# Six half-size weight tiles, one line for loads and crossings in the planner, a third U bank, and half of x over the crossbar

## The chip, the cores and the metric

The kernel runs on one core of a Trainium2 chip. The metric is device time of one execution in microseconds (us). The core has a matrix engine (PE, with its weight loads listed as PEld), a vector engine (DVE), an activation engine (ACT), a small-vector engine (POOL), and a queue engine (SP) that issues most transfers. ACT issues transfers too. A *crossing* below is a transfer that transposes 16-bit data on its way from one on-chip buffer to another.

## The reference

A four-layer decoder trunk over 256 tokens of width 1024, all in float32. Each layer has a token mixer of its own kind, then a gated feed-forward block, then a gated per-layer embedding:

```
for i in range(4):
    h = rmsnorm(x, ln_mix_pre[i])
    y = (rglru_block, dilated_attention, stick_breaking_attention, differential_attention)[i](h)
    x = x + rmsnorm(y, ln_mix_post[i])
    h = rmsnorm(x, ln_ffn_pre[i])
    x = x + rmsnorm((silu(h @ w_in[:, :2816]) * (h @ w_in[:, 2816:])) @ w_out, ln_ffn_post[i])
    gate = sigmoid(x @ w_ple_gate[i] + b_ple_gate[i])
    x = x + rmsnorm(gate * (p[i] @ w_ple_proj[i]), ln_ple[i])
```

The mixers have 16 heads of 64 (the fourth pairs them into 8); all projections are 1024 wide, qkv 3072. About 233 MB of weights are read once.

## The kernel before

**Two halves.** The tokens are split into two halves of 128 rows. Each half is a generator (`half(0)`, `half(1)`) that walks through all four layers and asks for weight slices one after another. Half 1 runs `LAG` = 11 slices behind half 0, so that one half's matmuls can fill the time in which the other normalises, transposes or takes its softmax.

**Weights.** A chunk is 1 MB of weights: four slices of 128 x 512. A raw tile holds one chunk, and there are `RAWRING` = 3 raw tiles. `Weights.load` starts the transfers of chunks ahead: column chunks of one or two pieces, row chunks in one transfer of 1 MB, the last row chunk of a matrix in two. `Weights.ensure` works by units of half a chunk (two slices): ACT copies the unit rounded to the fast matmul format into a `hi` tile, DVE subtracts to get a `lo` tile, and a ring of `RING` = 9 such pairs feeds the matmuls. A product is three matmuls of 512 columns: hi x hi, hi x lo, lo x hi (`mm3`). A raw tile is free for the next chunk when both of its units are split. Two chunks (`NATIVE`) are not split.

**Transposes of x.** `to_hT` needs x with the feature on the partition, as eight blocks of 128 x 128, and is called 22 times: before each of three attentions, four feed-forward blocks and four embeddings, for both halves. Blocks 0 to `XX` - 1 go over PE (`split_T`: matmuls with the identity into a `psT` bank), the others two at a time over the crossbar (`cross_T`: DVE copies the 16-bit halves apart into `planes`, ACT or SP issues the transposing transfer into `turned`, DVE copies back). `parts` then makes hi (ACT) and lo (DVE) of each block. With `XX` = 6, blocks 0 to 3 are one PE group, blocks 4 and 5 a second, and blocks 6 and 7 one crossing. Gated activations (`GBY`) and x (`XBY`) cross from ACT's queue, attention weights (`PBY`) from SP's.

**PSUM.** There are eight banks: four in `psY` (outputs), two in `psU` (products on their way: gated columns, q and k, v, attention outputs, the embedding's projection), two in `psT` (transposes).

**Order.** All instructions are recorded first, with their dependences, and `schedule` then plans an order for every engine by list scheduling over 24 rounds. Its prices are in `price` and `delay`; `Wires.land` says when a transfer lands. Before, a crossing issued by ACT lands 5250 ns after its start and takes no room; one from SP moves the shared line to at least 3750 ns after its start and adds 450; plain loads share that line.

Of the kernel before, what the change touches and what calls it, by code (L numbers as in the profile page):

```python
# [11 lines left out]
F32 = mybir.dt.float32  # L12
# [8 lines left out]
P = 128  # L21
# [11 lines left out]
LAG = 11  # L33
LOOK = 2
RING = 9
RAWRING = 3
PIECES = ((0, 256), (256, 512), (512, 1024))
LAST_PIECES = ((0, 512), (512, 1024))
WARM = 26
XX = 6  # L40
XQK = 0
XP = 4
GBY = 0
# [7 lines left out]
NATIVE = (0, 6)  # L51
# [198 lines left out]

XBAR_ISSUE = 1250
XBAR_LAND = 4000

# [14 lines left out]
class Wires:  # L270
# [3 lines left out]
        self.busy = 0.0  # L274

    def land(self, eng, op, t, size):
        if op == "dma_start_transpose":
            if eng == "ACT":
                return t + XBAR_ISSUE + XBAR_LAND
            self.busy = max(self.busy, t + XBAR_ISSUE + XBAR_LAND - 1500) + 450  # L280
            return self.busy + 1050
        self.busy = max(self.busy, t + DMA_FIRST) + size / DMA_RATE
        return self.busy + DMA_TOLD

# [33 lines left out]
def delay(a, b, op=None):  # L318

    if op == "dma_start_transpose":  # L320
        return XBAR_LAND
    if a == "SP":
# [99 lines left out]
class Weights:  # L422
# [29 lines left out]

        self.add("rows_n", w[k0 * P:(k0 + 2) * P, :].rearrange("(k p) n -> p k n", p=P))

    def load(self, upto):
        while self.nraw <= upto and self.nraw < len(self.chunks):
            if self.nraw in NATIVE:
                self.nraw += 1
                continue
            kind, what = self.chunks[self.nraw]  # L460
            r = self.raw_pool.tile([P, 4, 512], F32, tag="raw", name=f"raw{self.nraw}")
            if kind == "cols":
                for off, n, ap in what:
                    self.nc.sync.dma_start(out=r[:, :, off:off + n], in_=ap)
            elif kind == "rows":
                self.nc.sync.dma_start(out=r.rearrange("p (k c) n -> p k (c n)", k=2), in_=what)
            else:
                for c in range(2):
                    self.nc.sync.dma_start(out=r[:, 2 * c:2 * c + 2, :], in_=what[:, :, c * 512:(c + 1) * 512])
            self.raw[self.nraw] = r  # L470
            self.nraw += 1

    def ensure(self, slot, look=LOOK):
        last = min(slot // 2 + look, 2 * len(self.chunks) - 1)
        while self.nunit <= last:
            u = self.nunit
            self.nunit += 1
            self.units.pop(u - RING, None)
            if u // 2 in NATIVE:

                t = self.split_pool.tile([P, 2, 512], F32, tag="hi")
                for off, n, ap in self.chunks[u // 2][1]:
                    self.nc.sync.dma_start(out=t[:, :, off:off + n], in_=ap[:, 2 * (u % 2):2 * (u % 2) + 2, :])
                self.units[u] = (t, None)
                continue
            self.load(u // 2 + RAWRING - 1)
            r = self.raw[u // 2][:, 2 * (u % 2):2 * (u % 2) + 2, :]
            hi = self.split_pool.tile([P, 2, 512], F32R, tag="hi", name=f"hi{u}")
            lo = self.split_pool.tile([P, 2, 512], F32R, tag="lo", name=f"lo{u}")
            self.nc.scalar.copy(out=hi, in_=r)  # L490
            self.nc.vector.tensor_tensor(out=lo, in0=r, in1=hi, op=ALU.subtract)
            self.units[u] = (hi, lo)
# [6 lines left out]
def trunk(ctx, tc, a, out):  # L499
    nc = Program(tc)  # L500
    sb = ctx.enter_context(tc.tile_pool(name="sb", bufs=1))
    ps = ctx.enter_context(tc.tile_pool(name="ps", bufs=1, space=PSUM))
    pool = lambda name, bufs, real=sb: Ring(nc, name, bufs, real)
    cp = pool("cp", 1)
    raw_pool = pool("rawp", RAWRING)
    split_pool = pool("splitp", RING)
    gp = pool("gp", 3)
    ap = pool("ap", 1)
    tp_ = pool("tp", 2)
    psY = pool("psY", 4, ps)  # L510
    psU = pool("psU", 2, ps)
    psT = pool("psT", 2, ps)
    wp = pool("wp", 1)


# [111 lines left out]
    for i in range(DEPTH):  # L627
        if i == 0:
            add_out(a["a_w_out"][0], KT)
        else:  # L630
            n = "abcd"[i]
# [40 lines left out]
    def split_T(src, hi, lo, nblk, g=None):  # L672

        t = psT.tile([P, 512], F32, tag="t")
        for b in range(nblk):
            TE.transpose(t[:, b * P:(b + 1) * P], src[:, b * P:(b + 1) * P], ident)
        parts(t[:, 0:nblk * P].rearrange("p (b c) -> p b c", c=P), hi, lo, g)
# [19 lines left out]
    def to_hT(h, g=None):  # L697

        hi, lo = alloc_hT(h)
        gk = lambda k: None if g is None else g[:, k]  # L700
        for k0 in range(0, XX, 4):
            k = slice(k0, min(k0 + 4, XX))
            split_T(x[h][:, k.start * P:k.stop * P], hi[:, k, :], lo[:, k, :], k.stop - k0, gk(k))
        for k0 in range(XX, KT, 2):
            k = slice(k0, k0 + 2)
# [619 lines left out]
```

## Time and profile before

| | |
|---|---|
| median of 3 runs | 1306.0 us (1304.79 to 1307.13) |
| profiled execution, its own time | 1309.04 us |
| span of the profile | 1307.2 us |
| mean granted PE clock | 0.998 |
| PE busy | 1285.9 us, 98% |
| DVE busy | 992.4 us, 76% |
| ACT busy | 755.4 us, 58% |
| read from memory | 233.92 MB, 180 GB/s over the span |

The profiled execution ran 1.84 us longer than the span from its first to its last instruction. A busy PE is not PE at its peak: matmuls overlap in the records, and small pauses between them are counted in. What a stage is short of is read from windows of time and from the waits, not from the shares over the whole span.

### The profile page before, as it was taken

The numbers are of one execution on the slowest core, as the hardware profiler recorded it, in microseconds if no ns is written. First come the engines' busy times: TensorE is split into PE (matmuls) and PEld (weight loads), VectorE is DVE, ScalarE is ACT, GpSimd is POOL, SyncE is SP. The second block draws the span as 40 slices with busy tenths as digits, with TensorE's granted clock in tenths as the row PEclk, the third lists the DMA queues.
The fourth block names the chain that finished last, engine by engine and source line by source line (L and its number), as shares of the span: only waits on it lengthen the run. The fifth ranks groups of instructions, "written<-read, shape, count | busy, mean of one in ns | idle before, by whom it ended". The sixth has DMA issues, their size and how long they took to land.

```text
span 1307.2 us, 16953 instructions
## 1 busy us (share of the span) xinstructions
PE 1285.9 (98%) x6062; PEld 1033.0 (79%) x6062; DVE 992.4 (76%) x1760; ACT 755.4 (58%) x1300; POOL 35.6 (3%) x62
## 2 busy tenths in 40 slices
PE   9999999999999999999999999999999999999997
PEld 8977888887777888888777788888877777888886
DVE  7999666689986766668888876666889878666675
ACT  8985444466865644445667564444567766444453
POOL 1000000001000000000000000000000000000000
PEclk9999999999999999999999999999999999999999
DMA  9368677676678866667667777667666558667661
GB/s 346 125 207 219 207 208 203 204 214 201 166 203 184 229 204 198 199 206 232 199 162 173 195 222 209 202 196 203 222 199 189 141 151 230 209 209 205 205 195 36
DMA packets 257332, 258.37 MB, mean 198 GB/s; under 512 B 99296, under 2 KB 216288, under 8 KB 257248
## 3 DMA queue, kind: packets, MB, share of 16 engines
q1 hardware_dynamic: 197408, 242.86, 60.6%
q10 hardware_dynamic: 59840, 14.43, 6.7%
q8 instruction: 47, 0.77, 0.3%
q14 instruction: 37, 0.30, 0.1%
HBM read 233.92 MB, written 1.05 MB: 180 GB/s over the span
## 4 chain that ended last, share of the span: by engine, by line
PE 70%; DVE 13%; DMA 7%; ACT 7%; issue 2%; POOL 0%; SPq 0%; ACTq 0%; POOLq 0%; DVEq 0%
PE psU_u_n L178 43%; PE psY_y_n L178 26%; DVE splitp_lo_n L178 5%; DVE w_n L178 4%; DMA xp_turned_n<-xp_planes_n 4%; ACT w_n L178 2%; ACT splitp_hi_n L178 2%; DMA rawp_raw_n<-in_a_w_in_dram 2%; DVE ap_t_n L178 1%; ACT L178 1%; PE psT_t_n L178 1%; DVE cp_x_n L178 1%; DVE xp_planes_n L178 1%; DVE ap_hTlo_n L178 1%; DMA rawp_raw_n<-in_c_w_qkv_dram 1%
## 5 line engine op out<-in xcount | busy, mean ns | idle before, releaser
L178 DVE TENSOR_TENSOR splitp_lo_n<-rawp_raw_n,splitp_hi_n 128x1024 fp32r<-128x1024 f32 x420 | 511.5, 1221 | 165.7 <-ACT splitp_hi_n L178 162.7
L178 ACT CAST splitp_hi_n<-rawp_raw_n 128x1024 fp32r<-128x1024 f32 x420 | 436.3, 1046 | 213.7 <-PE psU_u_n L178 124.7
L178 PE MATMUL psU_u_n<-splitp_hi_n,ap_hThi_n 128*128 128x512 f32 x992 | 395.1, 399 | 1.5 <-ACT ap_B_n L178 1.1
L178 PE MATMUL psU_u_n<-splitp_lo_n,ap_hThi_n 128*128 128x512 f32 x992 | 393.9, 397 | 0.0
L178 PE MATMUL psU_u_n<-splitp_hi_n,ap_hTlo_n 128*128 128x512 f32 x992 | 392.5, 397 | 0.1
L178 PEld LDWEIGHTS psU_u_n<-splitp_hi_n,ap_hThi_n 128*128 128x128 f32 x992 | 186.9, 188 | 49.2 <-issue 3.5
L178 PEld LDWEIGHTS psU_u_n<-splitp_hi_n,ap_hTlo_n 128*128 128x128 f32 x992 | 186.5, 188 | 45.5 <-DVE ap_hTlo_n L178 1.4
L178 PEld LDWEIGHTS psU_u_n<-splitp_lo_n,ap_hThi_n 128*128 128x128 f32 x992 | 186.9, 188 | 43.6 <-DVE splitp_lo_n L178 0.5
L178 PE MATMUL psY_y_n<-splitp_hi_n,y_n 128*128 128x512 f32 x352 | 137.1, 395 | 0.7 <-ACT y_n L178 0.7
L178 PE MATMUL psY_y_n<-splitp_hi_n,w_n 128*128 128x512 f32 x352 | 133.3, 397 | 0.0
L178 ACT ACTIVATE w_n<-psU_u_n,tp_sm_n 128x256 f32<-128x256 f32 (+1 forms) x96 | 47.2, 491 | 126.4 <-PE psU_u_n L178 81.1
L178 DVE SCALAR_TENSOR_TENSOR w_n<-psU_u_n,tp_sm_n,w_n 128x256 f32<-128x256 f32 x88 | 42.4, 483 | 64.1 <-ACT w_n L178 64.1
L178 PE MATMUL psY_y_n<-splitp_hi_n,ap_hThi_n 128*128 128x512 f32 x208 | 82.7, 401 | 1.2 <-DVE y_n L178 1.1
L178 PE MATMUL psY_y_n<-splitp_lo_n,ap_hThi_n 128*128 128x512 f32 x208 | 82.3, 398 | 0.0
L178 DVE COPY w_n<-xp_turned_n 128x512 uint16<-128x512 uint16 x150 | 68.1, 457 | 18.3 <-DMA xp_turned_n<-xp_planes_n 18.3
L178 PE MATMUL psY_y_n<-splitp_hi_n,ap_hTlo_n 128*128 128x512 f32 x208 | 80.7, 397 | 0.0
L178 PEld LDWEIGHTS psY_y_n<-splitp_hi_n,y_n 128*128 128x128 f32 x352 | 66.0, 188 | 17.1 <-ACT y_n L178 1.1
L178 PEld LDWEIGHTS psY_y_n<-splitp_hi_n,w_n 128*128 128x128 f32 x352 | 65.9, 188 | 15.4 <-DVE w_n L178 0.2
L178 PE MATMUL psY_y_n<-splitp_lo_n,w_n 128*128 128x512 f32 x176 | 70.0, 398 | 0.0
L178 PE MATMUL psY_y_n<-splitp_lo_n,y_n 128*128 128x512 f32 x176 | 69.3, 394 | 0.0
L178 DVE COPY xp_planes_n<-w_n 128x512 uint16<-128x512 uint16 x148 | 61.5, 423 | 4.9 <-DMA xp_turned_n<-xp_planes_n 1.4
L178 POOL TENSOR_TENSOR tp_sm_n<-tp_sm_n,cp_half_neg_n 128x1 f32<-128x1 f32 (+1 forms) x44 | 31.5, 716 | 1130.3 <-DVE tp_sm_n L178 1130.3
(149 smaller groups left out, 1384.5 us busy)
## 6 DMA issues: line engine op xcount, KB each, us to landing
rawp_raw_n<-in_w_ffn_in_dram SPq DMA_DIRECT2D x176, 512.0 KB, 4.9
rawp_raw_n<-in_w_ffn_out_dram SPq DMA_DIRECT2D x40, 1024.0 KB, 4.9
rawp_raw_n<-in_w_ple_gate_dram SPq DMA_DIRECT2D x16, 1024.0 KB, 5.0
rawp_raw_n<-in_b_w_qkv_dram SPq DMA_DIRECT2D x16, 512.0 KB, 4.8
rawp_raw_n<-in_c_w_qkv_dram SPq DMA_DIRECT2D x16, 512.0 KB, 4.9
rawp_raw_n<-in_d_w_qkv_dram SPq DMA_DIRECT2D x16, 512.0 KB, 4.7
rawp_raw_n<-in_a_w_in_dram SPq DMA_DIRECT2D x6, 1024.0 KB, 9.5
rawp_raw_n<-in_w_ffn_out_dram SPq DMA_DIRECT2D x8, 512.0 KB, 4.7
```

Source lines behind the costliest of these rows:

```text
L178: getattr(engine.real, op)(*[self.bind(v) for v in args], **{k: self.bind(v) for k, v in kw.items()})
```

## The change

A raw tile now holds one unit (512 KB) instead of a chunk, and there are six instead of three: the same memory. `load` is replaced by `fetch(u, t)`, which starts the transfers of unit `u`, and is used for the unsplit units too; `ensure` fetches up to five units ahead of the one that it splits. A column chunk's piece of 512 KB becomes two of 256 KB, a row chunk of 1 MB two of 512 KB. `XX` becomes 4: blocks 4 and 5 of x go over the crossbar as blocks 6 and 7 do. `psU` gets three banks and `psT` one. In the planner every crossing, of either queue, starts on the shared line no sooner than 1180 ns after its issue, holds it for 870 ns, and is told 1700 ns later; the backward pass keeps its old prices.

```
-RAWRING = 3
+RAWRING = 6
-XX = 6
+XX = 4
+XBAR_FIRST, XBAR_TAKES = 1180, 870
+XBAR_TOLD = 1700
...
         if op == "dma_start_transpose":
-            if eng == "ACT":
-                return t + XBAR_ISSUE + XBAR_LAND
-            self.busy = max(self.busy, t + XBAR_ISSUE + XBAR_LAND - 1500) + 450
-            return self.busy + 1050
+            self.busy = max(self.busy, t + XBAR_FIRST) + XBAR_TAKES
+            return self.busy + XBAR_TOLD
...
+    def fetch(self, u, t):
+
+        kind, what = self.chunks[u // 2]
+        j = u % 2
+        if kind == "cols":
+            for off, n, ap in what:
+                self.nc.sync.dma_start(out=t[:, :, off:off + n], in_=ap[:, 2 * j:2 * j + 2, :])
+        elif kind == "rows":
+            self.nc.sync.dma_start(out=t.rearrange("p c n -> p (c n)"), in_=what[:, j, :])
+        else:
+            self.nc.sync.dma_start(out=t, in_=what[:, :, j * 512:(j + 1) * 512])
...
-            self.load(u // 2 + RAWRING - 1)
-            r = self.raw[u // 2][:, 2 * (u % 2):2 * (u % 2) + 2, :]
+            while self.nraw < min(u + RAWRING, units):
+                if self.nraw // 2 not in NATIVE:
+                    self.raw[self.nraw] = self.raw_pool.tile([P, 2, 512], F32, tag="raw", name=f"raw{self.nraw}")
+                    self.fetch(self.nraw, self.raw[self.nraw])
+                self.nraw += 1
+            r = self.raw.pop(u)
...
-    psU = pool("psU", 2, ps)
-    psT = pool("psT", 2, ps)
+    psU = pool("psU", 3, ps)
+    psT = pool("psT", 1, ps)
```

## Rows read from the trace of the kernel before

**Rows 1.** The page: span, and busy time of each engine.

```profile
span 1307.2 us, 16953 instructions
PE 1285.9 (98%) x6062; PEld 1033.0 (79%) x6062; DVE 992.4 (76%) x1760; ACT 755.4 (58%) x1300; POOL 35.6 (3%) x62
```

**Rows 2.** Stretches of 20 us; the first row names the columns.

```profile
core 0: us, PE busy (x) PEld busy (x) DVE busy (x) ACT busy (x) POOL busy (x), PEclk, DMA share, GB/s
0.00:20.00 20.00, 17.53 (x128) 17.09 (x129) 13.09 (x37) 14.31 (x26) 3.88 (x12) 1.00 0.90 325
140.00:160.00 20.00, 20.00 (x88) 16.09 (x87) 12.83 (x18) 9.07 (x12) 0.00 (x0) 1.00 0.64 191
300.00:320.00 20.00, 19.23 (x87) 15.30 (x86) 19.52 (x38) 13.47 (x25) 2.26 (x2) 1.00 0.63 201
320.00:340.00 20.00, 19.63 (x105) 15.13 (x104) 19.30 (x61) 17.11 (x49) 0.93 (x1) 1.00 0.58 174
420.00:440.00 20.00, 20.00 (x91) 16.12 (x90) 15.96 (x30) 14.32 (x26) 1.10 (x2) 1.00 0.71 198
640.00:660.00 20.00, 18.08 (x83) 14.46 (x83) 15.09 (x32) 12.73 (x30) 1.25 (x2) 0.91 0.69 196
700.00:720.00 20.00, 18.77 (x115) 14.15 (x115) 19.69 (x37) 14.44 (x24) 0.38 (x2) 1.00 0.67 146
960.00:980.00 20.00, 19.37 (x89) 15.42 (x88) 19.63 (x38) 13.48 (x26) 1.41 (x2) 1.00 0.63 197
1040.00:1060.00 20.00, 18.88 (x94) 14.31 (x93) 19.00 (x54) 14.32 (x43) 1.01 (x1) 1.00 0.89 184
```

**Rows 3.** The chain that ended last, in a feed-forward block: start, us, what.

```profile
114.92 9.78 PE psU_u_n L178 x42
...
131.70 9.80 PE psU_u_n L178 x42
```

**Rows 4.** The same chain: two PE transposes of x between matmuls.

```profile
616.81 0.22 PE psT_t_n L178 x2
```

**Rows 5.** Groups by line and tile: DVE's two copies of a crossing (count, busy us, mean ns).

```profile
L178 DVE COPY xp_planes_n<-cp_x_n 128x512 uint16<-128x512 uint16 x22 | 9.3, 421 | 0.1
L178 DVE COPY w_n<-xp_turned_n 128x512 uint16<-128x512 uint16 x150 | 68.1, 457 | 18.3 <-DMA xp_turned_n<-xp_planes_n 18.3
```

**Rows 6.** Waits of PE's weight loads: us in total, times, longest.

```profile
PEld psU_u_n L178 <- ACT ap_B_n L178: 2.5, 3, 1.3
PEld psU_u_n L178 <- DVE ap_t_n L178: 2.3, 2, 1.2
PEld psU_u_n L178 <- DVE ap_hTlo_n L178: 1.4, 4, 0.5
PEld psU_u_n L178 <- ACT w_n L178: 0.7, 2, 0.4
```

**Rows 7.** The chain that ended last: two loads on it in layer 2.

```profile
635.89 7.50 DMA rawp_raw_n<-in_c_w_qkv_dram
...
711.76 6.33 DMA rawp_raw_n<-in_c_w_out_dram
```

**Rows 8.** The tile `turned`: ACT's issues of crossings (min/median/max ns), and landings of all.

```profile
L178 ACTq DMA_TRANSPOSE xp_turned_n<-xp_planes_n x110: 1205/1207/2197, 89.8 to 1279.9; - x110
...
DMA to landing us min/median/max: 2.3/3.5/8.9
```

**Rows 9.** Transfers by line: count, KB each, median us from issue to landing.

```profile
rawp_raw_n<-in_w_ffn_in_dram SPq DMA_DIRECT2D x176, 512.0 KB, 4.9
rawp_raw_n<-in_w_ffn_out_dram SPq DMA_DIRECT2D x40, 1024.0 KB, 4.9
```

**Rows 10.** The raw tile: SP's issues of one matrix's loads (min/median/max ns).

```profile
L178 SPq DMA_DIRECT2D rawp_raw_n<-in_w_ffn_in_dram x176: 367/499/1536, 74.5 to 1221.9; - x176
```

**Rows 11.** What SP's queue waited for: us in total, times, longest.

```profile
SPq L178 <- DVE splitp_lo_n L178: 524.5, 118, 12.8
```

**Rows 12.** The chain that ended last: a crossing of attention weights in layer 1.

```profile
391.07 8.90 DMA xp_turned_n<-xp_planes_n
```

More of the change, by code (lines that the diff above doesn't have):

```diff
@@ L453, in add_rows_n @@
         self.add("rows_n", w[k0 * P:(k0 + 2) * P, :].rearrange("(k p) n -> p k n", p=P))
[L455 to L471, printed above, removed]
+    def fetch(self, u, t):
[8 more added lines that the diff above has]
+            self.nc.sync.dma_start(out=t, in_=what[:, :, j * 512:(j + 1) * 512])
     def ensure(self, slot, look=LOOK):
-        last = min(slot // 2 + look, 2 * len(self.chunks) - 1)
+        units = 2 * len(self.chunks)
+        last = min(slot // 2 + look, units - 1)
         while self.nunit <= last:
@@ L481, in ensure @@
                 t = self.split_pool.tile([P, 2, 512], F32, tag="hi")
-                for off, n, ap in self.chunks[u // 2][1]:
-                    self.nc.sync.dma_start(out=t[:, :, off:off + n], in_=ap[:, 2 * (u % 2):2 * (u % 2) + 2, :])
+                self.fetch(u, t)
                 self.units[u] = (t, None)
                 continue
-            self.load(u // 2 + RAWRING - 1)
-            r = self.raw[u // 2][:, 2 * (u % 2):2 * (u % 2) + 2, :]
+            while self.nraw < min(u + RAWRING, units):
[4 more added lines that the diff above has]
+            r = self.raw.pop(u)
             hi = self.split_pool.tile([P, 2, 512], F32R, tag="hi", name=f"hi{u}")
```

## The prediction

> **What bounds the kernel now.** Begin with the page. PE is busy 98% of the span, DVE 76% [rows 1]: whatever is gained has to be gained on PE's own time or in the few places where PE stands. Then cut the time into stretches. In the feed-forward blocks PE is busy 20.00 of 20 us while DVE and ACT have 13 and 9 [rows 2]; the chain there is matmuls alone, and repeats every 16.78 us for 48 + 24 = 72 matmuls of 512 columns, 0.233 us each [rows 3]. No edit of buffers or transfers shortens that. The pauses are where a layer begins or its attention runs: PE lacks 0.77 and 0.37 us in the first two stretches of layer 1, 0.63 in layer 3, with DVE at 19.3 to 19.6 of 20; 1.92 and 1.23 us in layer 2; 1.12 us late in layer 3 [rows 2]. So the change can act on three things: work that PE no longer does, waits that end in a load or a crossing, and waits for a free U bank. Against them stands what it adds to DVE, ACT and the transfer engines.
>
> All terms are set against the profiled execution's 1309.04 us (1307.2 of span and 1.84 around it). That run lies 3.0 us above the median of 1306.0, so the sum is carried over to the median as a difference. About 0.2% (2.6 us) is what a measurement of this kernel can tell from no change.
>
> **PE work removed.** 22 calls of `to_hT` each lose two PE transposes. Two take 0.22 us on the chain [rows 4], so 22 x 0.22 = 4.8 us. Where DVE is the short engine, PE time saved buys nothing: I take out the six calls ahead of attention and the two of layer 0, and count 14 x 0.22 = 3.1. Bounds: 0 and 4.8.
>
> **DVE work added.** Each call gains one crossing, so a copy apart of 0.421 and a copy back of 0.457 us [rows 5], 0.88 us; hi and lo of the blocks are made as before. With DVE at 13 to 16 of 20 us this is covered by PE's matmuls. Where DVE is at 19.3 or more (layers 1 and 3, two calls each) the cover is gone: 4 x 0.88 = 3.5; with layer 0's two calls 5.3. PE still has 96 to 98% there [rows 2], so a DVE delay is paid only in part. I take +2.6, half of the upper bound; bounds 0 and 5.3.
>
> **The crossing's latency and its issue.** Blocks 4 and 5 are wanted two slices, 2 x 3 x 0.233 = 1.4 us, before blocks 6 and 7, which already cross today. On ACT's queue the second crossing stands behind the first, whose issue takes 1.21 us [rows 8]; what waits behind both is ACT's `hi` copies, the sum of squares for the norm, and then DVE. So a call's last block may be 1.4 + 1.2 = 2.6 us tighter. The eight feed-forward calls have the least cover, since the other half then has only its lag of 11 slices left: upper bound 8 x 2.6 = 20.8 us. Lower bound nothing: today PE's weight loads for U wait only 1.4 us in all, four times, for the `lo` of x [rows 6], and the stretch in which half 1 of layer 1 enters its block shows PE at 20.00 [rows 2]. I take +2.0, near the rows.
>
> **Raw tiles.** SP's queue sits waiting for DVE's split 524.5 us in 118 waits [rows 11]: a load is issued when a raw tile comes free, not when the line is free. Today the tile comes free after its second unit; half tiles come free after each, and a unit no longer waits for the other unit's bytes. Where this counts is layer 2: a load of 7.50 us stands on the chain, issued late behind DVE, and one of 6.33 us before the output projection [rows 7]. The first costs PE 1.92 us of standing, and behind it the granted clock of that stretch is 0.91 [rows 2]: 0.09 x 20 = 1.8 us more, PE running for 3.6 us at 1.2 instead of 2.4 GHz after it stood. The second is in the stretch that lacks 1.23 us. Together 4.9 us is the upper bound of the gain, 0 the lower (another wait right behind). I take -3.5: the tile is free about one split sooner, and half the bytes land first; what is late next is DVE's own queue. The price is more transfers: the 176 loads of one matrix become 352, at 0.50 us of SP's queue each [rows 10], 88 us more, spread over a queue that waits six times as long. Crossings of attention weights queue on SP too, so a load that waits for its tile holds them up, as it does now.
>
> **The planner's line.** Crossings land after 3.5 us in the median, at worst 8.9 [rows 8]; the old model says 5.25 for ACT's, unloaded or not. The long ones stand on the chain: 8.90 us in layer 1 [rows 12], and the stretch late in layer 3 lacks 1.12 us at a transfer share of 0.89 [rows 2]. A plan that puts loads and crossings in one line places fewer consumers ahead of what they wait for. Upper bound of the gain: 2 x 1.12 = 2.2, the second 1.12 for layer 1's spot. A new order can also be worse by about as much. I take -1.0.
>
> **PSUM.** Three rows of PE's waits for U name the evictions that free a bank: `v` by ACT (2.5), the embedding's product by DVE (2.3), ACT's copies (0.7), 5.5 us in all [rows 6]. A third bank removes the cause; some of the time goes to DVE, which is behind in the same stretches. I take -3.5; bounds 0 and 5.5. The single `psT` bank I cost at nothing: with four PE blocks x fills one bank where six filled two, so a call of `to_hT` leaves no fewer banks than now. If that doesn't hold, x and the other half's q and k queue for the one bank, and each waits for the other's evictions on ACT and DVE.
>
> **Sum.** -3.1 + 2.6 + 2.0 - 3.5 - 1.0 - 3.5 = -6.5 us: 1302.5 for the profiled execution, 1299.5 for the median, 0.5% less.
>
> **The rivals.**
> *Slower: x arrives late.* The eight feed-forward calls show their full latency, because half 1's lag doesn't grow with it. The sign turns where a call costs (6.5 + 2.0) / 8 = 1.06 us instead of the 0.25 that I take. At 1.7 us, two thirds of the 2.6, it is 13.6 - 8.5 = +5.1: 1311. For it: the second issue of 1.21 us and the crossing's worst landing of 8.9 [rows 8]. Against it: 1.4 us of waits in all today [rows 6]. The Trainium skill, in "VectorE: DVE Perf Modes" (Rules for kernel authors), says to transpose 128 x 128 on TensorE where PSUM will do as the destination, and to use the crossbar otherwise; by it this edit goes the wrong way, and no row here shows the two paths side by side for the same block.
>
> *The same: smaller transfers carry less.* In the first 20 us 325 GB/s go at a share of 0.90, 361 at a full share; in the feed-forward block, with pieces of 512 KB in short rows, 191 at 0.64, 298 at a full share [rows 2], 17% less. If halving the pieces cost the same again, the start, where the share is 0.90, would need 20 / 0.83, 4.1 us more; the steady part, at 0.64, would hide it. Then -6.5 + 4.1 = -2.4: 1303.6. Against it: 512 KB and 1024 KB land in the same 4.9 us [rows 9], so size isn't what they wait for. The Trainium skill's "DMA: Bandwidth & Descriptors" (Rules for kernel authors) asks for at least 1 MiB per transfer for the best bandwidth, and the change goes from there to 512 and 256 KB; by the landings in the trace the rule doesn't bite between 512 and 1024 KB, and 256 KB is not shown.
>
> *The same: the next wait takes the place.* Loads and U banks are freed, but DVE, at 19.3 to 19.6 of 20 in those stretches [rows 2], is what ends last anyway: the two terms of -3.5 fall away, and +0.5 remains: 1306.5.
>
> *All of it.* Every term at its better bound: -4.8 - 4.9 - 2.2 - 5.5 = -17.4, nothing paid: 1288.6.
>
> **How the numbers follow.** The forecast gets 0.48, "all of it" 0.14, smaller transfers 0.08, the next wait 0.12, x late 0.18. So faster 0.62, same 0.20, slower 0.18. The forecast's own range is 1295 to 1303; the range given goes from 1290, which leaves out about half of "all of it", to 1310, which leaves out the worse half of the late x.
>
> **What would show it.** Right: in layer 2's first stretch PE near 20 and its clock at 1.00; no 7.50 us load on the chain; waits of U for `v`, the embedding's product and ACT's copies under 2 us together; 44 transposes of x fewer; the matmuls' period unchanged at 16.78 us. Wrong: PE standing at the start of the feed-forward blocks behind a `lo` or `hi` of x; DVE's share at 20 in layers 1 and 3 with PE lower than today; the first weights later than now; PE's transposes waiting for evictions of `psT`.

## The result and the profile after

| | before | after |
|---|---|---|
| median | 1306.4 us (4 runs beside those of after) | 1315.0 us (1313.7 to 1316.8, 4 runs) |
| ratio | | 1.0065, 95% interval 1.0048 to 1.0082 |
| forecast | | 1299.5, range 1290 to 1310 |

The kernel became 8.7 us slower; the prediction has the wrong sign and its range doesn't hold the time. The profiled execution of after took 1316.8 us.

The page of after, its span and busy time [rows 1]:

```profile
span 1315.0 us, 17797 instructions
PE 1285.8 (98%) x6018; PEld 1027.2 (78%) x6018; DVE 1005.9 (76%) x1804; ACT 753.5 (57%) x1298; POOL 36.9 (3%) x62
```

PE issues 44 instructions fewer, and DVE 44 more: these are the transposes that went and the two copies of 22 crossings, as predicted. DVE's busy time grew by 13.5 us. PE's busy time is the same although it has less to do, and the span is 7.8 us longer: what grew is time in which PE stands or runs slowly. The period of a feed-forward block did not move (16.78 us before [rows 3]); the chain that ended last has it at 16.76 us, six rounds in 100.53:

```profile
797.44 9.78 PE psU_u_n L178 x42
...
897.97 9.78 PE psU_u_n L178 x42
```

Stretches of 20 us, where PE lost and where it won (0 to 20, 640 to 660 and 700 to 720 stand in [rows 2] for before):

```profile
core 0: us, PE busy (x) PEld busy (x) DVE busy (x) ACT busy (x) POOL busy (x), PEclk, DMA share, GB/s
0.00:20.00 20.00, 16.75 (x125) 16.26 (x126) 12.66 (x36) 14.50 (x27) 4.08 (x12) 1.00 0.91 326
100.00:120.00 20.00, 17.41 (x75) 13.10 (x73) 16.48 (x38) 10.26 (x20) 0.66 (x1) 1.00 0.79 184
260.00:280.00 20.00, 18.62 (x82) 14.64 (x81) 13.64 (x24) 10.85 (x17) 0.55 (x1) 1.00 0.76 178
...
440.00:460.00 20.00, 18.68 (x81) 14.72 (x79) 14.74 (x25) 11.30 (x19) 0.55 (x1) 1.00 0.90 225
600.00:620.00 20.00, 18.60 (x82) 14.71 (x82) 15.82 (x25) 11.25 (x21) 0.55 (x1) 1.00 0.64 187
...
640.00:660.00 20.00, 19.52 (x92) 14.90 (x90) 17.62 (x32) 13.93 (x27) 1.41 (x2) 1.00 0.77 225
700.00:720.00 20.00, 20.00 (x119) 15.38 (x118) 18.77 (x41) 16.06 (x29) 0.80 (x3) 1.00 0.80 227
```

Before, the four stretches of loss were:

```profile
100.00:120.00 20.00, 19.33 (x87) 15.22 (x86) 18.42 (x52) 12.16 (x21) 0.55 (x1) 1.00 0.83 210
260.00:280.00 20.00, 20.00 (x91) 16.12 (x90) 16.41 (x25) 12.11 (x19) 0.55 (x1) 1.00 0.67 211
440.00:460.00 20.00, 20.00 (x87) 16.00 (x86) 14.15 (x23) 9.74 (x14) 0.00 (x0) 1.00 0.85 236
600.00:620.00 20.00, 20.00 (x94) 16.16 (x93) 18.65 (x31) 12.05 (x21) 1.10 (x2) 1.00 0.84 256
```

Layer 2 is mended as predicted: 640 to 660 went from 18.08 to 19.52 and its clock from 0.91 to 1.00, and 700 to 720 from 18.77 to 20.00. The new losses lie elsewhere, at the seams of the stages: where half 1 enters its block in layer 0 (100 to 120), in layer 1's block (440 to 460), and where a block passes into the embedding (260 to 280, 600 to 620). DVE is far from full there, 13.6 to 16.5 of 20. So no engine became the bound; something stands.

What stands shows in the list of waits (us in total, times, longest), here rows of DVE, ACT and PE's weight loads:

```profile
DVE w_n L178 <- DMA xp_turned_n<-xp_planes_n: 36.7, 39, 3.0
...
PEld psT_t_n L178 <- DVE cp_x_n L178: 7.0, 6, 1.8
...
ACT y_n L178 <- DMA w_n<-in_p_dram: 6.0, 4, 1.6
...
ACT w_n L178 <- DMA w_n<-in_p_dram: 4.2, 3, 2.6
...
PEld psU_u_n L178 <- ACT ap_hThi_n L178: 3.8, 8, 1.8
PEld psU_u_n L178 <- DVE ap_hTlo_n L178: 3.4, 8, 0.9
...
PEld psU_u_n L178 <- ACT ap_B_n L178: 1.6, 5, 0.4
...
PEld psU_u_n L178 <- ACT w_n L178: 0.7, 2, 0.4
```

Two of these waits, before:

```profile
DVE w_n L178 <- DMA xp_turned_n<-xp_planes_n: 18.3, 15, 3.7
...
ACT w_n L178 <- DMA w_n<-in_p_dram: 0.5, 1, 0.5
```

DVE's wait for a crossing to land, ahead of the copy back, doubled: 18.3 us in 15 waits, now 36.7 in 39. The crossings themselves land no later: 2.3/3.6/8.6 us least, median and most, where it was 2.3/3.5/8.9 [rows 8]. DVE arrives at them sooner. One such place is the timeline of DVE from 108 to 115 us; the bracket is idle time and what ended it:

```profile
108.46 0.20 DVE L178 TENSOR_SCALAR w_n<-w_n 128x64 f32<-128x64 f32 x1
110.30 0.45 DVE L178 COPY w_n<-xp_turned_n 128x512 uint16<-128x512 uint16 x1 [1.64 <-DMA xp_turned_n<-xp_planes_n]
110.65 1.21 DVE L178 TENSOR_TENSOR splitp_lo_n<-rawp_raw_n,splitp_hi_n 128x1024 fp32r<-128x1024 f32 x1
111.78 0.42 DVE L178 TENSOR_TENSOR y_n<-w_n,y_n 128x256 fp32r<-128x256 f32 x1
113.83 0.84 DVE L178 COPY w_n<-xp_turned_n 128x512 uint16<-128x512 uint16 x2 [1.63 <-DMA xp_turned_n<-xp_planes_n]
```

DVE works through its list in order. The first stand is for a gated crossing, and behind it waits a weight split that doesn't need it; the second is for x's own two crossings, whose copies go into the `hi` and `lo` that follow. ACT had issued all three in a row from 103.86 us on. PE shows the bill at once: from one matmul's start to the next it takes 1.61 us at 109.63, where it waits for the gated product itself, and 1.71 us at 113.06, where it waits for a `hi` of x, instead of 0.233.

The second wait is ACT's for the plain load of `p`, the embedding's input: 0.5 us before, 10.2 in the two rows now. It stands ahead of the seams into the embedding. In 260 to 280 us ACT, DVE and PE have, in this order:

```profile
273.41 0.41 ACT L178 CAST y_n<-w_n 128x256 fp32r<-128x256 f32 x1 [1.62 <-DMA w_n<-in_p_dram]
...
276.27 1.54 DVE L178 SCALAR_TENSOR_TENSOR cp_x_n<-ap_t_n,tp_sm_n,cp_x_n 128x256 f32<-128x256 f32 x3
...
276.81 0.83 PE L178 MATMUL psT_t_n<-ident,cp_x_n 128*128 128x128 f32 x4 [1.38 <-DVE cp_x_n L178]
```

Behind ACT's copy of `p` stands the sum of squares for the norm that ends the block, behind that DVE's update of x, and PE's transposes wait for x. The same happens in the other three layers (1.40, 0.74 and 1.23 us of PE; 4.75 us in all four). In these four places `p` lands 4.1 to 4.9 us after its issue, where before it took 2.1 to 2.2.

### The profile page after: what moved, and what is told of

It reads as the page before. It is cut to its first block, busy times and chain, and to the rows that moved or that the text cites. A ratio compares the mean times of both kernels' runs of the same rounds, so it can differ in the third digit from the quotient of the medians.

```text
span 1315.0 us, 17797 instructions
## 1 busy us (share of the span) xinstructions
PE 1285.8 (98%) x6018; PEld 1027.2 (78%) x6018; DVE 1005.9 (76%) x1804; ACT 753.5 (57%) x1298; POOL 36.9 (3%) x62
## 4 chain that ended last, share of the span: by engine, by line
PE 41%; DVE 4%; DMA 3%; ACT 2%; issue 1%; POOL 0%; ACTq 0%; POOLq 0%; DVEq 0%; SPq 0%
PE psU_u_n L178 27%; PE psY_y_n L178 13%; DMA xp_turned_n<-xp_planes_n 2%; DVE splitp_lo_n L178 2%; DMA w_n<-in_p_dram 1%; DVE w_n L178 1%; PE psT_t_n L178 1%; ACT splitp_hi_n L178 1%; DVE cp_x_n L178 1%; DVE xp_planes_n L178 0%; ACT w_n L178 0%; POOL tp_sm_n L178 0%; DVE ap_hTlo_n L178 0%; DVE ap_t_n L178 0%; ACT ap_hThi_n L178 0%
## 5 line engine op out<-in xcount | busy, mean ns | idle before, releaser
L178 DVE COPY w_n<-xp_turned_n 128x512 uint16<-128x512 uint16 x172 | 78.6, 459 | 37.2 <-DMA xp_turned_n<-xp_planes_n 36.7
L178 PEld LDWEIGHTS psY_y_n<-splitp_hi_n,y_n 128*128 128x128 f32 x352 | 66.1, 188 | 17.9 <-ACT y_n L178 1.7
```

The costliest lines, as they stand in the source:

```text
L178: getattr(engine.real, op)(*[self.bind(v) for v in args], **{k: self.bind(v) for k, v in kw.items()})
```

## The experiments

The expectations call the theories by short names. PROMISE says that the new line in the planner promises landings sooner than the chip delivers them, so that the order puts waiting copies ahead of work that is ready. BUF says that x's second crossing waits for a landing buffer shared with the gated crossings. The others are named in the texts. All ratios are against the kernel before.

**The four parts, each alone.** `only_tiles` has the changed `Weights` class and six raw tiles. `only_x`, `only_line` and `only_psum`:

```
-XX = 6
+XX = 4
```
```
-            if eng == "ACT":
-                return t + XBAR_ISSUE + XBAR_LAND
-            self.busy = max(self.busy, t + XBAR_ISSUE + XBAR_LAND - 1500) + 450
-            return self.busy + 1050
+            self.busy = max(self.busy, t + XBAR_FIRST) + XBAR_TAKES
+            return self.busy + XBAR_TOLD
```
```
-    psU = pool("psU", 2, ps)
-    psT = pool("psT", 2, ps)
+    psU = pool("psU", 3, ps)
+    psT = pool("psT", 1, ps)
```

> The kernel before with the six half tiles alone. The prediction's term: -3.5 us, 1302 to 1304. Theory SP (the pauses ahead of the embedding come from the p load queued on SP behind a raw load that waits for its tile): slower by 3 to 7 us, with ACT waiting over 1 us for p at each of the four layers. Theories LINE and X: within 2 us of before, p within 0.5 us of ACT's need.

Measured: 1302.3 us, 0.9974 (0.996 to 0.9987).

> The kernel before with half of x over the crossbar alone. The prediction's terms together: -3.1 + 2.6 + 2.0 = +1.5 us. Theory X (the second crossing and its place in ACT's queue are the loss): slower by 5 to 10 us, with PE's waits for the hi and lo of x going from some 3 to over 8 us. Theories SP and LINE: within 3 us of before.

Measured: 1320.2 us, 1.0103 (1.0086 to 1.012).

> The kernel before with the planner's new line alone. The prediction's term: -1.0 us. Theory LINE (crossings of ACT's queue are promised 3.75 us after issue instead of 5.25, and DVE, which works in order, stands more behind those that land late): slower by 3 to 8 us, DVE's waits for crossings going from 18 us to 35 or more. Theories SP and X: within 2 us of before.

Measured: 1306.8 us, 1.0003 (0.9994 to 1.0013).

> The kernel before with three U banks and one T bank alone; x still takes two groups of PE transposes, now through one bank. The prediction's term: -3.5 us, waits of U's weight loads for v, the embedding's product and ACT's copies going from 5.5 to under 2 us. A rival, the single T bank as the loss: slower by 2 us or more, 1.2 us of it ahead of the first product, with PE transposes waiting for evictions of T.

Measured: 1303.6 us, 0.9977 (0.9964 to 0.9989).

Added up, -4.3 + 13.6 + 0.2 - 3.0 = +6.5 (medians against the 1306.6 of before in these runs): x would be the culprit, and the line harmless. Theory LINE fell for the line alone, whose DVE waits are 22.6 us and not 35; so did theory SP (`p` behind raw loads) for the tiles alone: ACT waits 2.6 us for `p`, and the time fell. Rows of PE's weight loads in `only_x` point at x too:

```profile
PEld psU_u_n L178 <- DVE ap_hTlo_n L178: 6.7, 10, 2.2
PEld psU_u_n L178 <- ACT ap_hThi_n L178: 6.1, 5, 2.9
...
PEld psY_y_n L178 <- ACT ap_hThi_n L178: 2.9, 5, 1.3
...
PEld psY_y_n L178 <- DVE ap_hTlo_n L178: 0.4, 2, 0.2
```

They add up to 16.1 us of waits for hi and lo of a transposed input, where before had 1.4 us for `lo` at U [rows 6] and 1.7 us for both at the outputs.

**The whole without x.** The counter-test:

```
-XX = 4
+XX = 6
```

> The changed kernel with x back to six blocks on PE. If the parts add up: 1306.5 - 3.4 (tiles) - 3.0 (PSUM) + 0.2 (line) = 1300. If the parts only look good alone, and what slows the changed kernel is their joint order: 1305 or more.

Measured: 1316.0 us, 1.0076 (1.0058 to 1.0094). With x back on PE the time is as bad as with the whole change. My reading of the four single runs fell: the parts don't add.

**What x costs by itself.** `x_twice` keeps `XX` = 6 and issues a crossing of blocks 4 and 5 besides, whose result isn't used; `x_own` is `only_x` with landing tiles of x's own; `x_early` is `only_x` with the second half of x updated first.

```
+        for k0 in range(4, XX, 2):
+            t = s256("gg").rearrange("p (b t) -> p b t", b=2)
+            cross_T(x[h][:, k0 * P:(k0 + 2) * P], t, by=(A, nc.sync)[XBY])
```
```
-            t = s256("gg").rearrange("p (b t) -> p b t", b=2)
+            t = wp.tile([P, 256], F32, tag="xown", bufs=2).rearrange("p (b t) -> p b t", b=2)
```
```
-PIECES = ((0, 256), (256, 512), (512, 1024))
+PIECES = ((512, 1024), (0, 256), (256, 512))
```

> The kernel before; blocks 4 and 5 of x go over PE as before and are used from there, and go over the crossbar too, into a tile that nobody reads. Theory WORK (DVE's two copies, ACT's issue, the transfer, the buffers they take): slower by 8 to 14 us, as with half of x over the crossbar. Theory LATE (the blocks come too late for the matmuls): within 4 us of before. Theory BUF (the landing tile's ring of two, shared with the gated columns and p): slower by 5 to 14 us, since the tile is taken all the same.

Measured: 1312.0 us, 1.004 (1.0025 to 1.0056).

> Half of x over the crossbar alone, but the crossings of x land in two tiles of their own instead of the ring of two that the gated columns and p use. Theory BUF: most of the 13.6 us come back, 1306 to 1311. Theories LATE and WORK: 1317 to 1322, no change.

Measured: 1318.7 us, 1.0094 (1.0077 to 1.0111).

> Half of x over the crossbar alone, but the update of x writes its second half first, so that the crossings can start some 1.0 us sooner and the PE blocks come last. Theory LATE: 3 to 8 us of the 13.6 come back, 1312 to 1317, and PE's waits for hi and lo of x fall from 16 to under 12 us. Theories WORK and BUF: 1318 to 1322.

Measured: 1322.3 us, 1.0117 (1.0067 to 1.0167).

The crossing as added work costs 5.3 us (1312.0 - 1306.65), between what WORK and LATE expected; buffers of its own give back 1.6 of 13.6, so BUF falls; an earlier second half shows no gain, and its runs spread from 1313.9 to 1328.8. No theory came out whole. What the three kernels with half of x on the crossbar share is that PE waits longer for hi and lo of a transposed input than the 3.1 us of before: 16.1 us, 11.9 with buffers of its own, 17.9 with the earlier half. `x_twice`, where nothing waits for the added crossing's result, has 8.2.

**Which pairs.** Half tiles with the PSUM part; the change without the line:

```
-            self.busy = max(self.busy, t + XBAR_FIRST) + XBAR_TAKES
-            return self.busy + XBAR_TOLD
+            if eng == "ACT":
+                return t + XBAR_ISSUE + XBAR_LAND
+            self.busy = max(self.busy, t + XBAR_ISSUE + XBAR_LAND - 1500) + 450
+            return self.busy + 1050
```

> Half tiles and PSUM's banks, without the planner's line and without more of x on the crossbar. Theory PROMISE (with small loads on the line the planner promises ACT's crossings after 3.8 us instead of 5.25, the chip delivers as before, and what waits in order behind them stands): the two gains of 3.4 and 3.0 add up, 1299 to 1302. Rival DRAW (every edit only draws another order, good or bad by up to 8 us): anything from 1298 to 1314, most likely 1304 to 1310.

Measured: 1303.1 us, 0.997 (0.9956 to 0.9985).

> The changed kernel with the old promise for crossings. PROMISE: gated crossings late by over 0.5 us against the plan fall from 26 to under 10; the time is that of the other three parts, 1306.5 - 6.4 and at most the 13.6 of x: 1306 to 1312, below the changed kernel's 1315. DRAW: no better than 1315 to be expected.

Measured: 1306.0 us, 0.9994 (0.9981 to 1.0007).

This is the turn. Undoing the line alone gives back 9.0 us of the changed kernel (1315.0 to 1306.0), though the line alone cost 0.2. Without x it costs 13.0 (1316.0 against 1303.1). And x beside tiles and PSUM costs 2.9, not 13.6. `tiles_psum` itself came out 1.1 us above what PROMISE expected: the gains of tiles and PSUM don't add up.

**What the line needs.** The kernel before with half tiles and line, and with line and PSUM part (the diffs above):

> The kernel before with the half-size raw tiles and the planner's line, two U banks and XX = 6. Theory PROMISE (with half-size loads the shared line promises crossings about 1.5 us sooner than the chip lands them, so orders get too tight): the line costs here about what it cost the after kernel and the kernel without x, so 1302.3 + 9 to 13 = 1311 to 1315, and gated crossings land later than planned by over 0.5 us in 20 or more of 88. Rival BANK (the loss needs the single psT bank or the third U bank beside the line): no loss, 1302 to 1304.

Measured: 1318.8 us, 1.0089 (1.0074 to 1.0104).

> The kernel before with the planner's line and the PSUM change, raw tiles of 1 MB and XX = 6. Theory PROMISE: large loads still hold the line, crossings are promised near 4.6 us as with the line alone, so the line costs nothing beside PSUM: 1302 to 1305. Rival BANK: 1311 or more, with PE waiting for a psT or a U bank where it did not with the PSUM change alone.

Measured: 1307.0 us, 1.000 (0.999 to 1.001).

BANK falls, and PROMISE holds for the pair, with more than it expected: the line and the half tiles together cost 16.5 us over the tiles alone, with two U banks and x on PE. `line_psum` is 2 us above the range that PROMISE gave it, and 3.4 above `only_psum`. In the waits of `tiles_line` and then of `line_psum` the crossing's row is:

```profile
DVE w_n L178 <- DMA xp_turned_n<-xp_planes_n: 42.8, 40, 3.7
```
```profile
DVE w_n L178 <- DMA xp_turned_n<-xp_planes_n: 22.7, 28, 1.8
```

The worst place of `tiles_line`, in DVE's timeline and then in PE's:

```profile
107.25 0.20 DVE L178 TENSOR_SCALAR w_n<-w_n 128x64 f32<-128x64 f32 x1
111.12 0.45 DVE L178 COPY w_n<-xp_turned_n 128x512 uint16<-128x512 uint16 x1 [3.67 <-DMA xp_turned_n<-xp_planes_n]
111.47 0.18 DVE L178 TENSOR_SCALAR w_n<-w_n 128x64 f32<-128x64 f32 x1
111.57 1.63 DVE L178 SCALAR_TENSOR_TENSOR ap_hTlo_n<-psT_t_n,cp_par_n,ap_hThi_n 128x128 fp32r<-128x128 f32 x6
```
```profile
107.59 0.39 PE L178 MATMUL psU_u_n<-splitp_lo_n,ap_hThi_n 128*128 128x512 f32 x1
111.96 0.79 PE L178 MATMUL psU_u_n<-splitp_hi_n,ap_hTlo_n 128*128 128x512 f32 x1 [3.98 <-DVE ap_hTlo_n L178]
```

Six `lo` copies of x, which PE wants, stand behind a copy back of a gated product that lands 7.82 us after its issue at 103.28; the plan had promised 3.75. In the kernel before, the same gated product was promised after 5.25 us and landed after 5.74; its copy back stands behind all the `lo` of x, at 110.15 us, and DVE doesn't stand for it.

**Only the promise.** The changed kernel, and it without x, with one number put back near the old promise:

```
-XBAR_TOLD = 1700
+XBAR_TOLD = 3200
```

> The changed kernel with one number changed in the plan: a crossing on the line is told 3200 ns after it leaves it instead of 1700, so that none is promised in under 5.25 us. The program on the chip has the same instructions in another order. PROMISE: 1304 to 1311, ACT's and DVE's waits for crossings from 43 to under 30 us. DRAW: within 2 us of 1315, or anywhere.

Measured: 1310.5 us, 1.002 (1.0007 to 1.0034).

> The changed kernel with XX = 6 and crossings told 3200 instead of 1700 ns after the line has taken them, so that they are promised as late as before, near 5.25 us. Theory PROMISE: most of the 13.0 us that the line costs there comes back, 1303 to 1308. If the loss lies in anything else that the shared line does (crossings of ACT holding it against loads, loads held against them), it stays above 1311.

Measured: 1309.5 us, 1.0023 (1.0009 to 1.0037). In medians 4.5 of the 9.0 us that the line costs come back with x and 6.5 of 13.0 without, half each; 1309.5 is short of the 1303 to 1308 that PROMISE expected, and below the 1311 from which on the loss was to lie in anything else that the shared line does. The waits for the crossing fall to where they were before the change; in `no_x_told`:

```profile
DVE w_n L178 <- DMA xp_turned_n<-xp_planes_n: 15.3, 17, 2.3
```

**Is it one unlucky order?** The planner keeps the best of 24 plans. These keep another one, of rounds 8 to 23 (for `tiles_draw` of rounds 0 to 7):

```
-        if best is None or end < best[0]:
+        if r >= 8 and (best is None or end < best[0]):
```

> The changed kernel with the best of the planner's rounds 8 to 23 instead of 0 to 23: another order, whose planned end is 0.2 us later than that of the one taken. If the loss belongs to the change and its promises: 1312 to 1318. If it is the luck of one order: 1304 to 1311.

Measured: 1313.9 us, 1.0052 (1.003 to 1.0074).

> The kernel before with the best of the plans of rounds 8 to 23 instead of that of all 24 (modelled 1290.4 instead of 1289.7). It measures what another order of the same work alone does: PROMISE expects within 4 us of before, 1302 to 1310; if it moves by 8 us or more, the plan's luck alone could have made the result, and no single part could be blamed.

Measured: 1301.6 us, 0.9957 (0.9942 to 0.9972).

> Half-size raw tiles and the planner's line, with the best plan of rounds 8 to 23 (modelled 1293.8 instead of 1293.1). Theory PROMISE: the promise is as early in every order, so this one loses too: at least 8 us above the tiles alone (1302.3), that is 1310 or more, with gated crossings late by over 0.5 us in 20 or more of 88. Rival LUCK (one order among many was bad): another order falls within 5 us of the tiles alone, 1298 to 1307.

Measured: 1316.0 us, 1.007 (1.0047 to 1.0093).

> Half-size raw tiles alone, with the best plan of rounds 0 to 7 (modelled 1293.5) instead of that of round 23 (1292.8). It says how sure the gain of 3.4 us for the tiles is: if the gain is the tiles' own, 1299 to 1306; if it was the order's luck, it may lie anywhere from 1298 to 1311, and a time above 1306.4 would show that the tiles by themselves bring nothing that is larger than the spread between orders. PROMISE says nothing about this run beyond that it stays below 1310.

Measured: 1308.0 us, 1.0018 (1.0006 to 1.003).

Another order of the same instructions moves before by 5.3 us, more than the 4 that PROMISE allowed, and the tiles by 5.7 (1302.3 to 1308.0; 6.6 against the runs of before beside each). The loss is in both orders of the changed kernel and of tiles with line; the gain of the tiles alone is in one order and not in the other. Of all versions `before_draw`, `only_tiles`, `tiles_psum` and `only_psum` beat both kernels clear of the noise, at 1301.6 to 1303.6, and the quickest of them changes nothing but the draw.

**The promise against the landing.** For each kernel I replayed its planner and set the landing that the plan had given each of the 88 gated crossings, from its issue, beside the landing in the trace. Late means over 0.5 us later than promised. The third column is the row of DVE's waits for a crossing, in us.

```
                          late of 88   DVE's wait   median us
before                         3          18.3       1306.4
before_draw                    1           8.3       1301.6
only_tiles / tiles_draw      5 / 3     13.2 / 11.7   1302.3 / 1308.0
only_psum                      3          11.7       1303.6
tiles_psum                    10          12.8       1303.1
no_line                        5          15.6       1306.0
only_line                      3          22.6       1306.8
line_psum                      9          22.7       1307.0
tiles_line                    30          42.8       1318.8
tiles_line_draw               30          39.1       1316.0
no_x                          36          41.8       1316.0
after                         26          36.7       1315.0
after_draw                    20          23.6       1313.9
after_told / no_x_told       6 / 9     13.1 / 15.3   1310.5 / 1309.5
only_x                         5          29.0       1320.2
```

Each trace is of one execution; those of `only_tiles` (1308.3), `tiles_line_draw` (1310.6) and `after_told` (1314.2) lie 4 to 6 us off their medians. The kernels with half tiles and the new promise, 20 to 36 late, stand apart from all others, 1 to 10. DVE's wait by itself doesn't give the time: `after_draw` has 23.6 us of it and takes 1313.9, `only_line` 22.6 and 1306.8.

A crossing is promised 1180 + 870 + 1700 = 3750 ns when the planner's line is free. The median promise for ACT's crossings is 4.64 us in `only_line` and 3.75 in after, but early promises are not what half tiles add: 39 of the 88 gated crossings have one under 3.8 us in `only_line` too, against 46 in after. The difference is whether they are kept. In `only_line` the 39 landed after 2.4 us in the median and 2 of them late; of the 46, 11 were late in after and 16 in `tiles_line`. With loads of 1 MB the planner's line told rightly when a crossing goes through fast, with half tiles it did not; why is not shown. The promise and not a slower landing makes most of the late ones in after: 22 of its 26 would have been in time, within 0.5 us, for the old 5.25. Over all of ACT's crossings, x's included, the median landing hardly moved, 3.47 before and 3.67 after, with a tail to 8.6; 88% landed no later than 0.5 us after their promise before, 69% after. The plan thinks the change better by 4.1 us (1285.6 against 1289.7), while the chip is 8.7 slower.

## Why the prediction was wrong

**The failed step is the planner's line.** It said that a plan with loads and crossings in one line "places fewer consumers ahead of what they wait for", -1.0, with 2.2 as the bound either way. The runs show the opposite sign and several times the bound: +9.0 beside the other parts, +13.0 without x, +16.5 beside the tiles alone. The two orders of tiles and line lie 8.0 us or more above the two of tiles alone, whichever are compared; all five kernels with half tiles and the new promise took 1313.9 to 1318.8 us, all four with half tiles and the old one 1302.3 to 1308.0. The prediction set the median landing, 3.5, beside the promise of 5.25 and took the difference for slack. That slack was what covered most of the tail up to 8.9 [rows 8]. I also priced the part by itself, and by itself it came out near nothing (+0.2): its cost comes with the loads that another part made small. That the promise does it is shown by half: putting back the one number returns half the loss in both kernels, and the late crossings fall from 26 to 6 and from 36 to 9. But 4.5 and 6.5 us are each one order, and about the size of the spread between orders (5.3 and 5.7), and so is the other half, which stays open. A candidate for it is ACT's wait for `p`, 13.4 and 12.2 us in the two kernels; against it, `tiles_psum` has 11.3 and loses nothing.

The prediction held 2.6 us to be what a measurement can tell from no change. The spread between orders is twice that, larger than any of its terms.

**Raw tiles, -3.5.** Alone they measured -4.3 in one order and +2.4 in another; the mechanism in layer 2 is there: ACT's waits for loads of that matrix in 625 to 660 us, 3.0 us before, are gone, and the stretch is mended. The size is inside the spread of orders, so the term was neither shown nor refuted. The loads landed sooner. In after, 256 and 512 KB take 3.5 and 3.6 us where 512 and 1024 KB took 4.9 [rows 9]:

```profile
rawp_raw_n<-in_w_ffn_in_dram SPq DMA_DIRECT2D x352, 256.0 KB, 3.5
rawp_raw_n<-in_w_ffn_out_dram SPq DMA_DIRECT2D x88, 512.0 KB, 3.6
```

So the rival of smaller transfers that carry less falls: the first 20 us moved 326 GB/s at a share of 0.91, where it was 325 at 0.90. The rule of the Trainium skill that was weighed there ("DMA: Bandwidth & Descriptors", Rules for kernel authors, 1 MiB or more) doesn't bite in these runs. What no term of the sum held is the load of `p`, on the same queue: at the four seams it lands 3.1 to 3.8 us after its issue with half tiles alone, in two orders, but 3.1 to 4.0 with the PSUM part alone too, instead of 2.1 to 2.2; in after 4.75 us of PE's standing follow it. No run takes this wait away by itself, so neither its price nor its cause is shown.

**PSUM, -3.5.** Alone -3.0, with the waits of U for `v`, the embedding's product and ACT's copies at 0.8, none and 0.5, 1.3 us together where it was 5.5 [rows 6]; in after 1.6, none and 0.7. That is right to the sign, and alone under the 2 us that the prediction named, but the time is also within the spread of orders. Beside the tiles the two make -4.0, not -7. The single `psT` bank, costed at nothing, has at most a small price: with the PSUM part alone the first stretch has 17.24 us of PE instead of 17.53, and the transposes' 7.0 us of waiting in after are for x from DVE, not for an eviction. No run parts the two banks.

**x: -3.1 + 2.6 + 2.0 = +1.5.** Within the change it is -1.0 (after against `no_x`) and without the line +2.9: about as reckoned. Alone it is +13.6 (+12 to +16 with its variants), worse than the rival of the late x, which said +5.1, and with the waits that the rival named: PE's for hi and lo. A rule of the Trainium skill ("VectorE: DVE Perf Modes", Rules for kernel authors: transpose on TensorE when PSUM will do as the destination) spoke against the edit; `only_x` agrees with it at +13.6, the whole change against `no_x` doesn't. Why smaller loads and a third bank take most of that away is not settled: of 44 crossings of x 17 land late on the plan in `only_x` and 8 in `no_line`, but no run separates cause from order.

**The next wait takes the place** did not happen as told, since DVE is not fuller where PE stands; a wait did come, from the plan.

**The listed signs.** Right: layer 2 and its load, the 44 transposes, the period; the waits for a U bank only with the PSUM part alone. Of the wrong ones, PE standing for hi or lo came true in part (7.2 us at U instead of 1.4), and so did the later first weights: at 9.17 us PE stands 0.94 us for them, 0.20 before. DVE at 20 did not, and the transposes did not wait for `psT`.

## What to carry to other kernels

A planner's promised time for a transfer is a choice between slack and risk: on engines that work in order, a copy placed ahead of ready work pays every landing that is later than promised, and the tail of the landings counts, not their median. Whether a cost model got better is asked by setting each promise beside its landing in the trace, not by the plan's own end, which here improved by 4.1 us while the chip lost 8.7. Parts that change the sizes a planner sees have to be priced together with the planner's edit; and before a gain of 0.3% is put down to a part, run the same kernel in another order, which here moved it by 0.4%.

## What the runs showed of the hardware

After the pause of `tiles_line` at 107.6 us, PE runs at the lower of its two levels. Stretches of that kernel:

```profile
107.00:112.00 5.00, 1.02 (x6) 0.40 (x4) 1.30 (x7) 1.89 (x8) 0.00 (x0) 0.81 0.72 222
112.00:117.00 5.00, 5.00 (x12) 3.94 (x13) 4.11 (x14) 3.42 (x8) 0.55 (x1) 0.51 0.01 4
117.00:122.00 5.00, 5.00 (x24) 4.04 (x23) 3.66 (x7) 2.69 (x4) 0.00 (x0) 1.00 0.72 206
```

With PE busy for all 5.00 us it does 12 matmuls at a granted clock of 0.51 (1.2 GHz) and 24 at 1.00 (2.4 GHz): a stand of 4 us cost some 2.4 us more behind it (0.49 of the 5.00). In after, two stands of 1.6 and 1.7 us in 109 to 115 left the clock of their 20 us at 1.00. A crossing's landing is not a property of its size: the same 128 x 512 of 16 bits landed 2.3 to 9.6 us after issue across the kernels.
